# One level of Strassen's product in the odd layer's projections, early products at the layer change, and bias rows by head

## The chip, the core and the metric

The kernel runs on one core of a Trainium2 chip. The metric is the device time of one execution in microseconds; three runs of the kernel before took 2047.49, 2048.87 and 2050.56 us, median 2048.87. Engines: PE multiplies matrices and writes PSUM banks (128 x 512 numbers of 4 bytes); PEld loads the stationary side of a matmul; ACT, DVE and POOL work on elements; SP issues the transfers.

## What is computed

Two layers on 1024 tokens of 1024 features. The first, "even", layer mixes by moving averages, a retention recurrence and an attention over 256 memory rows. The second, "odd", layer is the one that the change rewrites:

```
u = rmsnorm(h, g)
q, kc, vc, ks, vs, kw, vw, gl, xq, gate = split_cols(u @ w_in, ODD_SPLITS)
c = nsa_attention(q, kc, vc, ks, vs, kw, vw, gl, ...)   # 12 heads, 2 groups of k and v
m = mem_attention(xq, mem_n, w_mem_kv)                   # 4 heads
y = concatenate([c, m]) * silu(gate)
return h + y @ w_out
```

The attention `nsa_attention` has three branches per head: over 63 compressed blocks (kc, vc), over the eight best blocks of 64 keys (ks, vs), and over a window of 512 keys (kw, vw), weighted by sigmoids of gl. A bias by distance, read from a small table, is added to the scores. A last rmsnorm gives the output.

## The kernel before

Activations lie transposed, features on the 128 partitions and tokens along the row, in two halves of 512 tokens. Each number is split into two parts, high (rounded to the fast matmul format) and low (the remainder), by `split`: ACT writes the high part (L68) and DVE, or POOL, the remainder (L69). A product of two such numbers takes three matmuls, high by high, high by low, low by high (`mm3`, L75 to L77).

`wload` (L82 to L89) fetches a weight block of 128 output columns, 1024 features deep, in one transfer of 512 KB and splits it whole; it has two buffers. `gemm` multiplies it with the eight feature tiles of u of one half, 8 x 3 matmuls of 128x512, into a bank called mm. `make_u` makes u of one half: it loads eight tiles, multiplies them with gains and the norm, and splits them.

The order: `mem_kv` projects the memory rows for the even layer; the even layer runs half by half and ends in `out_proj` (eight output blocks in two groups of features); u of the odd layer's first half is made; then, for the first half, kc and vc (`cmp_in`), the odd layer's memory projection, k and v (`kv_in`), the bias tables (`rel_tables`), the gate logits (`gates_in`), memory attention with q between (`mem_head`, `q_in`) and gates (`head_gates`); then u of the second half, the first half's memory output (`mem_out`), and the same projections again with `compress` and `select` between. Each weight block is thus fetched and split twice. k and v stay in SBUF, split; v is transposed by PE when it is made. q, gates and compressed probabilities go to DRAM.

`rel_tables` computes a row of 383 bias values for each of 12 heads and writes each row 128 times to DRAM in one transfer (L607), from which each head later reads a skewed table.

The attention then runs 24 units (half, head): `scores` of the next unit, `values` of this one and steps of the output projection `od_out` are interleaved by generators.

The code's order is a priority. A planner places instructions on the engines by its own simulated time, near the order of the code, when their inputs and buffers are free in that simulation. Each engine then runs its queue strictly in the planned order. Memory pools are stacks: a pool that opens takes the place of closed ones, and each of its tiles waits for the last readers of what lay there.

Of the kernel before, what the change touches and what calls it, by code (L numbers as in the profile page):

```python
# [9 lines left out]
F32 = mybir.dt.float32  # L10
# [8 lines left out]
T = 1024  # L19
# [13 lines left out]
HO = 4  # L33
PB = 2
# [4 lines left out]
def net(tc, a, out, dbg=None):  # L39
# [4 lines left out]
    def show(name, ap):  # L44
        if dbg is not None and name in dbg:
            sp.dma_start(dbg[name], ap)

    cst = ctx.enter_context(tc.tile_pool(name="cst", bufs=1))
    uc = ExitStack()
    wp = uc.enter_context(tc.tile_pool(name="wp", bufs=2, side="right"))  # L50
# [3 lines left out]
    pc_ = ExitStack()  # L54
    ps = pc_.enter_context(tc.tile_pool(name="ps", bufs=1, space=PSUM, reuse_waits="tile"))
    banks = {"mm": 3, "s": 2, "t": 2, "o": 1}

    def bank(tag, shape=(128, HT)):
        return ps.tile(list(shape), F32, name="ps_" + tag, tag=tag, bufs=banks[tag])

    def const(name, shape, eng=None):
        t = cst.tile(list(shape), F32, name="c_" + name)
        (eng or sp).dma_start(t, a[name])
        return t
# [9 lines left out]
    def mm3(o, wh, wl, xh, xl, start, stop):  # L74
        pe.matmul(o, wh, xh, start=start, stop=False)  # L75
        pe.matmul(o, wh, xl, start=False, stop=False)  # L76
        pe.matmul(o, wl, xh, start=False, stop=stop)  # L77
# [6 lines left out]
    def wload(src, n=1024, eng=None):  # L84
        r = wp.tile([128, n], F32, name="wr", tag="wr")
        sp.dma_start(r, src)
        h = wp.tile([128, n], F32R, name="wh", tag="wh")
        l = wp.tile([128, n], F32R, name="wl", tag="wl")
        split(h, l, r, eng=eng)  # L89
        return h, l  # L90

    def gemm(o, w, x, nk=8, c=128, start=True, stop=True):
        wh, wl = w
        for k in range(nk):
            mm3(o, wh[:, k * c:(k + 1) * c], wl[:, k * c:(k + 1) * c], x[k][0], x[k][1],
                start and k == 0, stop and k == nk - 1)

    gains = const("gains", (128, 4, 8))
# [9 lines left out]
    def add_square(acc, x, n, first, sq=None):  # L108
        if first:
            act.activation(acc, x, AF.Square)  # L110
        else:
            if sq is None:
                sq = tmp.tile([128, n], F32, name="sq", tag="uf", bufs=2)
            act.activation(sq, x, AF.Square)
            dve.tensor_tensor(acc, acc, sq, OP.add)

    def rstd_of(acc, n, keep=None):
        nt = n // 128
        ss = bank("t")
        for t in range(nt):  # L120
            pe.matmul(ss[:, t:t + 1], acc[:, t * 128:(t + 1) * 128], ones[:, 0:1], start=True, stop=True)
        rs = sm.tile([128, 4], F32, name="rs")
# [5 lines left out]
    def spread(rr, n, raw=False):  # L128
# [10 lines left out]
        r = tmp.tile([128, n], F32, name="rb", tag="rb")  # L139
# [3 lines left out]
    def rstd_rows(acc, n, raw=False):  # L143
        rr = rstd_of(acc, n)
        return spread(rr, n, raw), rr

    def make_u(srcs, n, gi, pool_, tag, rr=None):
# [5 lines left out]
        if rr is None:  # L153
            acc = tmp.tile([128, n], F32, name="acc", tag="acc")
            for k in range(8):
                add_square(acc, load(k), n, k == 0)
            rr = rstd_of(acc, n)
        rb = spread(rr, n)
# [9 lines left out]

    def mem_kv(p_, pre):
        w0 = wload(a[pre + "_mk"][0])  # L170
        acc = p_.tile([128, NMEM], F32, name="macc")
        u = []
        for k in range(8):
            x = p_.tile([128, NMEM], F32, name="mx", tag="mx", bufs=8 if pre == "ev" else 4)
            sp.dma_start(x, a["memT"][k])
            uh = p_.tile([128, NMEM], F32R, name="muh", tag="mu", bufs=16)
            ul = p_.tile([128, NMEM], F32R, name="mul", tag="mu", bufs=16)
            act.activation(uh, x, AF.Copy, scale=gains[:, 3, k:k + 1])
            dve.scalar_tensor_tensor(ul, x, gains[:, 3, k:k + 1], uh.bitcast(F32), OP.mult, OP.subtract)
            add_square(acc, x, NMEM, k == 0)  # L180
            u.append((uh, ul))
        if pre == "ev":
            sp.dma_start(ident, a["ident"])
        rb = None
        kd = [dr.tile([128, NMEM], F32, name=f"{pre}mkd{h}") for h in range(4)]
        vd = [dr.tile([128, HT], F32, name=f"{pre}mvd{m}") for m in range(2)]
        for h in range(4):
            w = w0 if h == 0 else wload(a[pre + "_mk"][h])
            o = bank("mm")
            gemm(o[:, :NMEM], w, u)  # L190
            if rb is None:
                rb, rr = rstd_rows(acc, NMEM)
            t = p_.tile([128, NMEM], F32, name="mkx", tag="mkx", bufs=4)
            act.copy(t, o[:, :NMEM])
            dve.tensor_tensor(t, t, rb, OP.mult)
            sp.dma_start(kd[h], t)
        o2 = [bank("mm"), bank("mm")]
        for c in range(4):
            wh, wl = wload(a[pre + "_mv"][c])
            for kk in range(2):  # L200
                k = 2 * c + kk
                for m in range(2):
                    mm3(o2[m], u[k][0][:, m * 128:(m + 1) * 128], u[k][1][:, m * 128:(m + 1) * 128],
                        wh[:, kk * 512:(kk + 1) * 512], wl[:, kk * 512:(kk + 1) * 512], k == 0, k == 7)
        for m in range(2):
            t = p_.tile([128, HT], F32, name="mvx", tag="mkx", bufs=4)
            act.activation(t, o2[m], AF.Copy, scale=rr[:, m:m + 1])
            sp.dma_start(vd[m], t)
        return kd, vd

    def load_mkv(kv, p_):
# [12 lines left out]
    def mem_att(w, u, mk, mv, h, p_, bufs=1):  # L224
# [35 lines left out]
    def gate_s1(w, u, p_, tag="s1", bufs=3):  # L260
        o = bank("mm")
        gemm(o, w, u)
        th = tmp.tile([128, HT], F32, name="th", tag="th", bufs=2)
# [5 lines left out]
    def make_y(p_, src, s1, scal, tag=None, bufs=0):  # L269
        y = (p_ if tag else tmp).tile([128, HT], F32, name="yf", tag=tag or "t2", bufs=bufs or 2)  # L270
        dve.scalar_tensor_tensor(y, src, scal, s1, OP.mult, OP.mult)
        return y

    def split_y(p_, y, bufs, eng=None, tag="yhl"):
        yh = p_.tile([128, HT], F32R, name="yh", tag=tag, bufs=bufs)
        yl = p_.tile([128, HT], F32R, name="yl", tag=tag, bufs=bufs)
        split(yh, yl, y, eng=eng)
        return yh, yl

    hp_ = [[dr.tile([128, HT], F32, name=f"hp{k}_{f}") for f in range(2)] for k in range(8)]  # L280
    hd = [[dr.tile([128, HT], F32, name=f"hd{k}_{f}") for f in range(2)] for k in range(8)]

    tmp = ctx.enter_context(tc.tile_pool(name="tmp", bufs=1))
    up = uc.enter_context(tc.tile_pool(name="up", bufs=1, side="right", reuse_waits="tile"))

    with tc.tile_pool(name="mk0", bufs=1, reuse_waits="tile") as mp_:
        mkv_ev = mem_kv(mp_, "ev")

    rh = []
    with ExitStack() as ec:  # L290
# [851 lines left out]
```

## Time and profile before

| | us |
|---|---|
| median of three runs | 2048.87 |
| lowest, highest | 2047.49, 2050.56 |
| span of the profiled execution | 2047.5 |
| PE busy in it | 1982.3 |
| DVE, ACT, POOL busy | 1164.9, 904.1, 404.0 |

The profiled execution's own time is its span, 2047.5 us from the first to the last instruction, 1.4 below the median. Matmuls are pipelined: one lasts longer than the distance to the next, and the groups' busy times add up overlaps. The price of a matmul in a gapless row is the distance between two starts. The granted clock is the share of full speed that PE was allowed.

### The profile page before, as it was taken

Reading aid. Unit: us, or ns where it says so; the run is one execution under the profiler, and the core shown is the slowest. Engines: PE = TensorE matmul, PEld = TensorE weight load, DVE = VectorE, ACT = ScalarE, POOL = GpSimd, SP = SyncE. Lnnn points to the kernel's source line nnn. Section 1 sums busy time; section 2 is a strip of 40 time slices with the busy share of each in tenths; the row PEclk is TensorE's granted clock in tenths of the full one; section 3 lists DMA queues with packets and bytes.
Section 4 is the critical chain, followed back from the end, with each engine's and each line's share of the span. In section 5 each row is a group of like instructions: output and inputs, shape, how many; then the busy total and the mean of one; then the engine's idle time right before and its main releaser. Section 6 shows DMA issues by size and latency. Waiting matters only on the chain.

```text
span 2047.5 us, 28222 instructions
## 1 busy us (share of the span) xinstructions
PE 1982.3 (97%) x10070; PEld 1657.5 (81%) x10070; DVE 1164.9 (57%) x2494; ACT 904.1 (44%) x1656; POOL 404.0 (20%) x478
## 2 busy tenths in 40 slices
PE   7999999999999999959999999999999999999996
PEld 6788888888888878748887888788788888888885
DVE  6674455746445573314444237744576677867675
ACT  5444222434421253313333222333576677767674
POOL 0130110013011000000002114300343444433422
PEclk9999999999999999979999999999899999999998
DMA  7433243632224365454356657444534532151312
GB/s 249 143 98 112 83 134 114 211 106 83 96 79 133 114 213 158 120 89 134 121 173 206 221 178 230 143 119 133 180 120 144 164 110 62 53 165 46 114 37 93
DMA packets 124051, 270.30 MB, mean 132 GB/s; under 512 B 15079, under 2 KB 31847, under 8 KB 123879
## 3 DMA queue, kind: packets, MB, share of 16 engines
q1 hardware_dynamic: 123912, 268.51, 42.5%
q8 instruction: 79, 1.29, 0.3%
q14 instruction: 60, 0.49, 0.1%
HBM read 217.87 MB, written 50.59 MB: 131 GB/s over the span
## 4 chain that ended last, share of the span: by engine, by line
PE 88%; DVE 4%; DMA 4%; issue 1%; ACT 1%; SPq 1%; POOL 0%; DVEq 0%; ACTq 0%; POOLq 0%
PE ps_mm L77 20%; PE ps_mm L75 20%; PE ps_mm L76 20%; PE ps_t L106 6%; PE ps_s L75 3%; PE ps_s L77 3%; PE ps_s L76 3%; PE ps_o L82 2%; PE ps_o L80 2%; PE ps_o L81 2%; PE ps_s L703 1%; DMA mkr<-odmkd 1%; DVE wl L69 1%; PE ps_o L75 1%; ACT wh L68 1%
## 5 line engine op out<-in xcount | busy, mean ns | idle before, releaser
L75 PE MATMUL ps_mm<-uh,wh 128*128 128x512 f32 (+1 forms) x1360 | 538.4, 396 | 25.8 <-ACT wh L68 25.6
L68 ACT CAST wh<-wr 128x1024 fp32r<-128x1024 f32 (+1 forms) x286 | 270.1, 947 | 631.3 <-PE ps_mm L76 505.2
L77 PE MATMUL ps_mm<-uh,wl 128*128 128x512 f32 (+1 forms) x1360 | 537.0, 395 | 3.3 <-DVE wl L69 3.3
L76 PE MATMUL ps_mm<-ul,wh 128*128 128x512 f32 (+1 forms) x1360 | 537.2, 395 | 1.2 <-DVE ul L69 1.2
L69 DVE TENSOR_TENSOR wl<-wr,wh 128x1024 fp32r<-128x1024 f32 (+2 forms) x222 | 277.7, 1251 | 348.5 <-ACT wh L68 347.5
L75 PEld LDWEIGHTS ps_mm<-uh,wh 128*128 128x128 f32 (+1 forms) x1360 | 255.5, 188 | 80.2 <-ACT wh L68 27.2
L77 PEld LDWEIGHTS ps_mm<-uh,wl 128*128 128x128 f32 (+1 forms) x1360 | 255.4, 188 | 58.4 <-DVE wl L69 5.6
L76 PEld LDWEIGHTS ps_mm<-ul,wh 128*128 128x128 f32 (+1 forms) x1360 | 255.4, 188 | 54.6 <-DVE ul L69 2.0
L77 PE MATMUL ps_mm<-yh,wl 128*128 128x512 f32 x512 | 206.9, 406 | 1.2 <-POOL wl L69 1.2
L75 PE MATMUL ps_mm<-yh,wh 128*128 128x512 f32 x512 | 204.1, 405 | 2.4 <-ACT yh L68 1.4
L76 PE MATMUL ps_mm<-yl,wh 128*128 128x512 f32 x512 | 205.1, 401 | 0.0
L69 DVE TENSOR_TENSOR apl<-ps_t,aph 128x512 fp32r<-128x512 f32 x204 | 136.2, 671 | 48.4 <-ACT aph L68 40.2
L69 POOL TENSOR_TENSOR wl<-wr,wh 128x512 fp32r<-128x512 f32 x64 | 84.5, 1324 | 383.0 <-PE ps_mm L76 295.1
L68 ACT CAST aph<-ps_t 128x512 fp32r<-128x512 f32 x204 | 114.3, 567 | 79.4 <-PE ps_o L81 41.7
L918 POOL TENSOR_TENSOR Pw<-Pw,arc 128x640 f32<-128x640 f32 (+2 forms) x96 | 97.3, 1014 | 141.0 <-DVE arc L914 67.8
L77 PEld LDWEIGHTS ps_mm<-yh,wl 128*128 128x128 f32 x512 | 96.7, 189 | 23.1 <-POOL wl L69 2.5
L75 PEld LDWEIGHTS ps_mm<-yh,wh 128*128 128x128 f32 x512 | 95.9, 189 | 23.0 <-ACT wh L68 2.0
L76 PEld LDWEIGHTS ps_mm<-yl,wh 128*128 128x128 f32 x512 | 96.9, 189 | 20.0 <-DVE yl L69 0.6
L910 ACT ACTIVATE Ps<-Ps,anm 128x512 f32<-128x512 f32 (+3 forms) x96 | 74.6, 777 | 33.4 <-DVE anm L907 33.0
L922 ACT ACTIVATE Ps<-Ps,arc 128x512 f32<-128x512 f32 (+3 forms) x96 | 74.5, 776 | 19.1 <-DVE arc L914 18.3
L106 PE MATMUL ps_t<-c_ident,Ps 128*128 128x128 f32 x432 | 67.9, 274 | 0.4 <-ACT Ps L922 0.4
L910 ACT ACTIVATE Pw<-Pw,anm 128x640 f32<-128x640 f32 (+2 forms) x96 | 65.6, 683 | 0.0
(316 smaller groups left out, 3297.0 us busy)
## 6 DMA issues: line engine op xcount, KB each, us to landing
wr<-in_ev_gate SPq DMA_DIRECT2D x32, 512.0 KB, 3.5
wr<-in_ev_out SPq DMA_DIRECT2D x32, 512.0 KB, 3.7
wr<-in_od_gate SPq DMA_DIRECT2D x32, 512.0 KB, 3.9
wr<-in_od_out SPq DMA_DIRECT2D x64, 256.0 KB, 3.0
oa<-oho SPq DMA_DIRECT2D x52, 256.0 KB, 2.2
oxr<-oa SPq DMA_DIRECT2D x52, 256.0 KB, 2.9
wr<-in_od_q SPq DMA_DIRECT2D x24, 512.0 KB, 3.6
x<-in_xT SPq DMA_DIRECT2D x32, 256.0 KB, 4.3
```

Source lines behind the costliest of these rows:

```text
L68: act.copy(hi, src)
L69: (eng or dve).tensor_tensor(lo, src, hi.bitcast(F32), OP.subtract)
L75: pe.matmul(o, wh, xh, start=start, stop=False)
L76: pe.matmul(o, wh, xl, start=False, stop=False)
L77: pe.matmul(o, wl, xh, start=False, stop=stop)
L80: pe.matmul(o, wh, xh, start=start, stop=False)
L81: pe.matmul(o, wl, xh, start=False, stop=False)
L82: pe.matmul(o, wh, xl, start=False, stop=stop)
L106: pe.transpose(o, x, ident[:k, :k])
L910: act.activation(pt, pt, AF.Exp, bias=nm[:, bi:bi + 1], accum_out=su[:, bi:bi + 1])
L918: pool.tensor_tensor(pt, pt, rc[:, bi:bi + 1].to_broadcast(list(pt.shape)), OP.mult)
L922: act.activation(pt, pt, AF.Copy, scale=rc[:, bi:bi + 1])
```

## The change

The odd layer's u of both halves is seen as a 2 x 2 matrix of blocks: B11 and B21 are the upper and lower 512 features of the first half, B12 and B22 those of the second. Two weight blocks of 128 columns (two heads) are likewise four blocks of 512 features. Instead of eight block products, seven are formed, from sums of blocks (Winograd's order of Strassen's product). The sums of u, T1 to T4, are made once; four sums of the weights, for each pair, on POOL. Products are added up in PSUM banks a, b and c, partly read out to SBUF between and combined there; results go to DRAM. All 22 pairs of blocks (6 q, 6 of k and v, 2 xq, 8 gate) go this way.

```diff
+    def u_sums(U, uo, x):
+        for k in range(4):
+            b11, b12, b22 = x[0][k], x[1][k], x[1][k + 4]
+            dve.tensor_tensor(b11, b12, b11, OP.subtract)
+            pool.tensor_tensor(b12, b22, b12, OP.subtract)
+            dve.tensor_tensor(b22, b22, b11, OP.subtract)
+            split(*U["T2"][k], b22)
...
+    def product(o, w, x, start):
+        for k in range(4):
+            c = slice(k * 128, (k + 1) * 128)
+            mm3(o, w[0][:, c], w[1][:, c], x[k][0], x[k][1], start and k == 0, k == 3, not start)
...
+    def strassen(U, sa, sb, sink, p_, scale=1.0, p1d=None):
...
+        pool.tensor_tensor(S[0], rb[:, lo], rb[:, hi], OP.add)
+        pool.tensor_tensor(S[1], S[0], ra[:, lo], OP.subtract)
+        pool.tensor_tensor(S[2], ra[:, lo], rb[:, lo], OP.subtract)
+        pool.tensor_tensor(S[3], ra[:, hi], S[1], OP.subtract)
...
+        pa = bank("a")
+        if p1d is None:
+            product(pa, whl(ra[:, lo]), U["B11"], True)
+            p1 = held(pa, "p1")
+            pc = bank("c")
+            product(pc, whl(ra[:, hi], pool), U["B21"], True)
+            done(0, 0, pc, p1)
+        else:
+            p1 = hold("p1")
+            sp.dma_start(p1, p1d)
+        product(pa, whl(S[1]), U["T2"], p1d is not None)
+        u2 = held(pa, "u2")
+        flush()
+        product(pa, whl(S[2]), U["T3"], False)
+        u3 = held(pa, "u3")
+        pb = bank("b")
+        product(pb, whl(S[0]), U["T1"], True)
+        done(1, 1, pb, u3)
+        product(pa, whl(rb[:, hi], pool), U["T4"], False)
...
+        def last():
+            product(pb, s4, U["B22"], False)
+            done(0, 1, pb, u2)
+
+        pending.append(last)
```

`held` copies a bank to SBUF (on ACT; on DVE, adding the first product, where that was held in DRAM), `done` adds a bank and a held tile on DVE and hands the result to a store or to the gate's tanh. `flush` issues the seventh product of the pair before. A weight is now fetched whole (`wraw`) and split in pieces of 512 (`whl`), of which five are buffered; the even layer's `wload` splits its 1024 in two pieces as well.

At the layer change, u of the first half is made before the even layer's last output projection, and then, while u of the second half is not there, the first two products of six pairs are formed from B11 and B21; the first is stored, the sum of both is a result:

```diff
+    ahead = [("kc", 0), ("vc", 0), ("q", 0), ("q", 2), ("q", 4), ("q", 6)]
...
+            kd[nm, i] = early(U, a["od_" + nm][i], sink,
...
+            if n == 0:
+                for k in range(8):
+                    sp.dma_start(X[1][k], hd[k][1])
+                    sp.dma_start(X[0][k], xd[k])
+        drain(mem_kv("od", None, u_late(uo), wtile("mrb")[:, :NMEM]))
+        u_half(U, X, 1, 1, rh[1], wtile("rb"))
+        u_sums(U, uo, X)
```

`mem_kv` now fetches the memory rows in two transfers through the weight buffers. The order of the odd layer becomes: pairs kc, vc, q 0, `rel_tables`, q 2, `compress`, q 4, the gate logits (for the second half from B11, T1 and B22), q 6 to 10, xq, `select`, gates 12 and 14, ks, and then kw, vs, vw and the gates 0 to 10 with a step of the memory attention before each. `mem_out` goes; its work is a generator in the attention stage. The bias rows go to DRAM once and are spread there, two heads at a time between pairs:

```diff
-                sp.dma_start(frd, fr[:, None, :383].to_broadcast([12, 128, 383]))
+            sp.dma_start(frs, fr)
...
+    def rel_rows(i):
+        for h in (2 * i, 2 * i + 1):
+            sp.dma_start(frd[h], frs[h:h + 1, :383].to_broadcast([128, 383]))
```

k and v are fetched from DRAM, split and transposed at the attention's start, group 0 before the first unit's scores and group 1 behind them:

```diff
+    def kv_prep(g):
+        for f in range(2):
...
+                k = fetch(tmp, zo["k" + br][g][f], "uf", 2, "kraw")
+                split(KT[br, g][0][:, c], KT[br, g][1][:, c], k)
+                v = fetch(tmp, zo["v" + br][g][f], "uf", 2, "vraw")
+                b = bank("t", (128, 4, 128))
+                for n in range(4):
+                    transpose(b[:, n], v[:, n * 128:(n + 1) * 128])
...
-        proj = [od_out(at, 1, {}, 0, (12, 13, 14, 15))]
+        proj = [od_out(at, f, {}, 0, (12, 13, 14, 15)) for f in range(2)]
```

The PSUM banks are laid out anew for the even layer, the pairs and the attention, and smaller buffers (in `compress` and `select` single instead of double) make room.

More of the change, by code (lines that the diff above doesn't have):

```diff
@@ L106, in transpose, with add_square @@
         pe.transpose(o, x, ident[:k, :k])
-    def add_square(acc, x, n, first, sq=None):
+    def add_square(acc, x, n, first, eng=None):
         if first:
@@ L126, in rstd_of, with spread @@
         return rr
-    def spread(rr, n, raw=False):
+    def spread(rr, n, raw=False, r=None):
         nt = n // 128
@@ L145, in rstd_rows, with u_pool, u_late, u_half @@
         return spread(rr, n, raw), rr
+    U_ORDER = ("T3", "T1", "T2", "B22", "B21", "B11", "T4")
+    def u_pool(uo, names=U_ORDER[:-1]):
+        return {nm: [[uo.tile([128, HT], F32R, name=f"{nm}{k}{s}", tag=f"{nm}{k}{s}") for s in "hl"] for k in range(4)]
+                for nm in names}
+    def u_late(uo):
+        return [[uo.tile([128, HT], F32R, name=f"T4{k}{s}", tag=f"T4{k}{s}") for s in "hl"] for k in range(4)]
+    def u_half(U, x, gi, f, rr, rb):
+        rb = spread(rr, HT, r=rb)
+        for k in range(8):
+            dve.scalar_tensor_tensor(x[f][k], x[f][k], gains[:, gi, k:k + 1], rb, OP.mult, OP.mult)
+            if f == 0 or k >= 4:
+                split(*U[("B11", "B21", "", "B22")[2 * f + k // 4]][k % 4], x[f][k])
@@ new lines, in product, with early @@
+    def product(o, w, x, start):
+        for k in range(4):
+            c = slice(k * 128, (k + 1) * 128)
+            mm3(o, w[0][:, c], w[1][:, c], x[k][0], x[k][1], start and k == 0, k == 3, not start)
+    pending = []
+    def early(U, sa, sink, hold, out_t, scale=1.0):
+        ra = wraw(sa)
+        pa = bank("a")
+        product(pa, whl(ra[:, :HT], pool), U["B11"], True)
+        t = hold()
+        act.activation(t, pa, AF.Copy, scale=scale)
+        pc = bank("c")
+        product(pc, whl(ra[:, HT:], pool), U["B21"], True)
+        d = dr.tile([128, HT], F32, name=f"p1d{len(kept)}")
+        kept.append(d)
+        sp.dma_start(d, t)
+        c = out_t()
+        dve.scalar_tensor_tensor(c, pc, scale, t, OP.mult, OP.add)
+        sink(0, 0, c, None)
+        return d
@@ new lines, in load_mkv @@
+    def load_mkv(kv, h, p_, bufs):
+        mk = p_.tile([128, 2, NMEM], F32R, name="mk", tag="mk", bufs=bufs)
+        mv = p_.tile([128, 2, 2, 128], F32R, name="mv", tag="mv", bufs=bufs)
+        t = p_.tile([128, 2, NMEM], F32, name="mkr", tag="xq", bufs=2)
+        sp.dma_start(t[:, 0], kv[0][h])
+        for m in range(2):
+            sp.dma_start(t[:, 1, m * 128:(m + 1) * 128], kv[1][m][:, h * 128:(h + 1) * 128])
+        split(mk[:, 0], mk[:, 1], t[:, 0])
+        v = t[:, 1].rearrange("p (m d) -> p m d", m=2)
+        split(mv[:, :, 0], mv[:, :, 1], v)
+        return mk, mv
@@ L167, in make_u, with load_mkv4 @@
         return u
[L169 to L211, printed above, removed]
+    def load_mkv4(kv, p_):
         mk = p_.tile([128, 4, 2, NMEM], F32R, name="mk", tag="mk")
@@ new lines, in net @@
+    wpx.close()
+    wpx = ExitStack()
+    cur["wp"] = wpx.enter_context(tc.tile_pool(name="wp", bufs=1, side="right", reuse_waits="tile"))
+    cur.update(wn=1024, wr=2, wh=5, ws=4, hs=4, sc=3, th=1)
+    uox = ExitStack()
+    uo = uox.enter_context(tc.tile_pool(name="uoA", bufs=1, side="right", reuse_waits="tile"))
+    U = u_pool(uo, ("B11", "B21"))
+    rb = spread(rh[0], HT, r=tm2.tile([128, HT], F32, name="rb", tag="rb"))
+    for k in range(8):
+        x = ep.tile([128, HT], F32, name="x0", tag="pa", bufs=3)
+        sp.dma_start(x, hd[k][0])
+        dve.scalar_tensor_tensor(x, x, gains[:, 1, k:k + 1], rb, OP.mult, OP.mult)
+        split(*U[("B11", "B21")[k // 4]][k % 4], x)
+        sp.dma_start(xd[k], x)
@@ L560, in od_out @@
                 if ct == 0:
-                    acc = tmp.tile([128, HT], F32, name="facc", tag="acc")
+                    acc = cur["late"].tile([128, HT], F32, name="facc", tag="acc")
                 add_square(acc, t, HT, ct == 0)
@@ new lines, in gates_in @@
+    def gates_in(p_):
+        w = wload(a["od_gl"], 288)
+        for f in range(2):
+            o = bank("s")
+            if f == 0:
+                gemm(o[:36], w, U["B11"] + U["B21"], c=36)
+            else:
+                gemm(o[:36], w, U["B11"], nk=4, c=36, stop=False)
+                gemm(o[:36], w, U["T1"], nk=4, c=36, start=False, stop=False)
+                gemm(o[:36], w, U["B22"], nk=4, c=36, start=False, k0=4)
+            gt = tmp.tile([36, HT], F32, name="gt", tag="uf", bufs=2)
```

814 lines of the change are left out of this document (487 added, 327 removed).

## The prediction

> **What bounds the kernel now.** I read the page's totals and its chain of waits first, then the busy time by stage, then the places where PE stood still.
>
> ```profile
> span 2047.5 us, 28222 instructions
> PE 1982.3 (97%) x10070; PEld 1657.5 (81%) x10070; DVE 1164.9 (57%) x2494; ACT 904.1 (44%) x1656; POOL 404.0 (20%) x478
> PE 88%; DVE 4%; DMA 4%; issue 1%; ACT 1%; SPq 1%; POOL 0%; DVEq 0%; ACTq 0%; POOLq 0%
> ```
>
> PE is busy 1982.3 of 2047.5 us and carries 88% of the chain. So PE work that is taken away counts in full wherever the stage around it is gapless. The next view, busy time in chosen stretches, says where it is (columns: stretch, length, then busy us and instructions of PE, PEld, DVE, ACT, POOL, granted clock, DMA share, GB/s).
>
> ```profile
> 0.00:60.00 60.00, 45.51 (x209) 35.68 (x210) 37.45 (x70) 32.89 (x58) 2.12 (x10) 0.97 0.79 252
> 60.00:735.00 675.00, 674.29 (x3162) 560.98 (x3162) 383.63 (x610) 241.59 (x388) 87.70 (x70) 1.00 0.36 114
> 735.00:830.00 95.00, 94.00 (x456) 77.77 (x456) 50.62 (x78) 38.59 (x58) 2.63 (x2) 1.00 0.65 203
> 883.00:925.00 42.00, 19.11 (x76) 15.55 (x75) 5.34 (x8) 5.12 (x9) 0.00 (x0) 0.67 0.57 105
> 1095.00:1120.00 25.00, 22.70 (x94) 17.05 (x93) 12.98 (x17) 7.03 (x11) 8.78 (x7) 1.00 0.78 242
> 1230.00:1310.00 80.00, 78.94 (x450) 68.30 (x449) 66.68 (x126) 23.80 (x36) 40.09 (x46) 1.00 0.64 199
> 1310.00:1436.00 126.00, 125.47 (x593) 104.03 (x592) 60.57 (x111) 46.63 (x89) 2.58 (x2) 1.00 0.43 129
> 1436.00:1456.00 20.00, 16.94 (x60) 12.98 (x59) 10.87 (x39) 11.49 (x30) 6.78 (x12) 0.74 0.61 198
> 1456.00:2005.00 549.00, 545.25 (x3216) 468.43 (x3215) 392.81 (x1216) 379.27 (x785) 220.33 (x298) 1.00 0.34 103
> ```
>
> The even layer (60 to 735) loses 0.71 us, the attention (1456 to 2005) 3.75 us: nothing is to be had there except work. PE stands still at the start (14.5 us of 60) and between 883 and 925 (22.9 us). The projections that the change rewrites lie from about 760 to 1436, and outside that hole they are gapless: even at 1230 to 1310, with DVE busy 66.68 of 80, PE lost only 1.06 us.
>
> **Term 1: fewer matmuls.** The odd layer projects 44 blocks of 128 columns (12 q, 12 of k and v, 4 xq, 16 gate) for two halves of the tokens, each in 8 x 3 matmuls of 128x512: 44 x 2 x 24 = 2112. After it are 22 pairs with 7 products of 4 x 3 matmuls: 22 x 7 x 12 = 1848. 264 go. A single matmul's duration overlaps the next, so the price is the distance of starts in a gapless row (timeline of PE, first and last of 14 matmuls):
>
> ```profile
> 1433.72 0.39 PE L76 MATMUL ps_mm<-ul,wh 128*128 128x512 f32 x1
> ...
> 1436.66 0.39 PE L77 MATMUL ps_mm<-uh,wl 128*128 128x512 f32 x1
> ```
>
> (1436.66 - 1433.72) / 13 = 0.2262 us; 264 x 0.2262 = **-59.7 us**. The busy column's 0.39 us would make it 103 us and be wrong. The Trainium skill, "TensorE: Matmul & The Clock Gate", section "Back-to-back issue gap", gives about 131 ns sustained and 215.7 ns isolated for 512 columns; as estimates by that page the term would be -34.6 or -56.9 us. No row here comes near 131 ns, so the measurement decides.
>
> **Term 2: the bias rows.** In the chain of waits the hole is one load of the memory keys, and the list of DMA issues shows what was in front of it.
>
> ```profile
> frd<-fr SPq DMA_DIRECT2D x1, 2298.0 KB
> 882.38 3.88 SPq L86
> 886.32 23.60 DMA mkr<-odmkd
> 890.00:895.00 5.00, 4.29 (x19) 3.21 (x18) 0.00 (x0) 0.00 (x0) 0.00 (x0) 1.00 0.68 81
> ...
> 915.00:920.00 5.00, 2.82 (x9) 2.44 (x10) 2.68 (x4) 3.16 (x6) 0.00 (x0) 0.50 0.23 51
> 920.00:925.00 5.00, 5.00 (x26) 4.31 (x25) 1.81 (x2) 1.16 (x3) 0.00 (x0) 0.93 0.84 299
> ```
>
> One issue of 2298 KB from twelve partitions moves at 70 to 80 GB/s, 31 us, and the small load behind it takes 23.60 us. Between the rows shown, 895 to 915, PE does nothing. Lost: 0.71 + 20 + 2.18, and at the low clock 2.82 x 0.5 + 5 x 0.07 = 1.8, together 24.7. Afterwards one row of 12x384 goes out and is spread in six calls of two heads, each behind a pair's loads, and the memory keys come much later. I take **-24.7 us**. Two heads are 383 KB; at the same 74 GB/s a call lasts 5.2 us, hidden by a pair of 84 x 0.2262 = 19.0 us of PE whose next weights have two buffers.
>
> **Term 3: what goes with the old order.** The second half's u (1095 to 1120, 2.3 us lost, with the weights of the output projection late) and the old layer change (735 to 830, 1.0 us) vanish: **-3.3 us**. The 96 matmuls of that half's memory output projection move into the attention and cost there what they cost here.
>
> **Term 4: added PE work.** The gate logits of the second half need 12 instead of 8 row blocks (B11, T1 and B22 instead of u): 12 more matmuls of 36 columns, spaced alike:
>
> ```profile
> 865.95 0.40 PE L75 MATMUL ps_mm<-uh,wh 128*36 128x512 f32 x1
> ...
> 868.04 0.40 PE L75 MATMUL ps_mm<-uh,wh 128*36 128x512 f32 x1
> ```
>
> 2.09 / 9 = 0.232; x 12 = **+2.8 us**.
>
> **Term 5: the pairs.** Prices, from the groups by form and the DMA issues:
>
> ```profile
> L68 ACT CAST wh<-wr 128x512 fp32r<-128x512 f32 x64 | 38.9, 616 | 44.8 <-PE ps_mm L76 16.6 <-DMA wr<-in_od_out 16.3 <-issue 7.9
> L620 ACT COPY kcx<-ps_mm 128x512 f32<-128x512 f32 x8 | 4.6, 579 | 0.0
> L556 DVE TENSOR_TENSOR oho<-ps_mm,oxr 128x512 f32<-128x512 f32 x64 | 43.7, 688 | 31.2 <-PE ps_mm L77 25.4 <-DMA oxr<-hd 4.6 <-DMA oxr<-oa 1.1
> L115 DVE TENSOR_TENSOR facc<-facc,sq 128x512 f32<-128x512 f32 x14 | 13.8, 983 | 8.0 <-ACT sq L114 7.9
> L115 DVE TENSOR_TENSOR acc<-acc,sq 128x512 f32<-128x512 f32 x14 | 9.6, 687 | 0.8 <-ACT sq L114 0.5
> L69 POOL TENSOR_TENSOR wl<-wr,wh 128x512 fp32r<-128x512 f32 x64 | 84.5, 1324 | 383.0 <-PE ps_mm L76 295.1 <-ACT wh L68 70.5 <-PE ps_mm L77 15.1
> wr<-in_od_q SPq DMA_DIRECT2D x24, 512.0 KB, 3.6
> aq<-qd SPq DMA_DIRECT2D x24, 256.0 KB, 2.8
> ```
>
> For 19.0 us of PE a pair asks: POOL 4 sums and 2 remainders, 6 x 1.32 = 7.9 us; ACT 7 splits at 0.62 and up to 3 copies at 0.58 (6.1), in a gate pair 4 tanh more (8.4); DVE 5 remainders at 0.69 and 4 combinations at 0.69 (6.2), in a gate pair 4 more (9.0). Weight loads fall from 88 of 512 KB to 44, and 6 for the early products; SP gains 46 stores of 256 KB (16 of k and v, 8 xq, 8 gates, 8 rows of u, 6 held products) and as many fetches later; with 38 fewer loads of 512 KB the queues carry less, under gapless PE. All engines stay under half of 19.0, so on average PE bounds. But bank a is read out after the third and the fourth product before the next may write it, and b has a single buffer. The order puts one other product, 12 x 0.2262 = 2.7 us, behind each of these reads (0.58 on ACT, 0.69 on DVE), and selection and memory attention share the queues in front of them. Bounds: nothing, as 1310 to 1436 (0.5 us in 126), and all three bare, 22 x (0.58 + 0.58 + 0.69) = 40.7 us. Nearest are the two gapless rows: 1.06 in 80 with DVE dense gives 22 x 19.0 / 80 x 1.06 = 5.5. I take **+5**.
>
> DVE's addition of two SBUF tiles took 983 ns in one group and 687 in another of the same shape. The Trainium skill, "GPSIMD Engine Reference", section "1. Specifications", says that GpSimd shares its SBUF interfaces with VectorE, and names contention with DVE instructions of two SBUF inputs. By that rule the five remainders of a pair would take 0.98, DVE 1.5 us more per pair; that alone stays hidden, yet it speaks against me where a read stands behind such a remainder.
>
> **Term 6: the layer change.** The first half's u is made under the last output projection (8 x 24 matmuls, 43.4 us); the twelve early products (32.6 us) and the odd memory projection (96 matmuls of 256 and 48 of 512 columns, 96 x 0.1131 + 48 x 0.2262 = 21.7 us) then cover the second half's load, u, and the sums: DVE 8 x 0.79 scalings and some 26 operations at 0.7, about 25 us, POOL about 16 us, loads of 4 MB (at 203 GB/s, the rate of the row from 735, 20 us). Behind them wait T2, then T3, T1, T4.
>
> ```profile
> L162 DVE SCALAR_TENSOR_TENSOR uf<-x,c_gains,rb 128x512 f32<-128x512 f32 x32 | 24.1, 790 | 2.0 <-ACT rb L140 2.0
> ```
>
> That is 25 of 54 us, early enough by half. What stays open is the change of weight buffers and banks, twice. If the cover went, these 25 us would come; the old change lost 1.0. I take **+4**.
>
> **Term 7: the start.** The memory rows now come through the two weight buffers, so the first key weights load only after four conversions and four squares:
>
> ```profile
> 4.91 1.04 ACT L68 CAST wh<-wr 128x1024 fp32r<-128x1024 f32 x1 [2.89 <-DMA wr<-in_ev_mk]
> 6.27 0.40 ACT L110 ACTIVATE macc<-mx 128x256 f32<-128x256 f32 x1
> L178 ACT ACTIVATE muh<-mx,c_gains 128x256 fp32r<-128x256 f32 x16 | 7.7, 498 | 5.3 <-DMA mx<-in_memT 5.3
> ```
>
> 4 x (0.50 + 0.40) + a load of 3.6 = about 7 us later; but in the first 60 us PE idles 14.5 anyway and splits of half a weight release matmuls earlier. Bounds -1 and +8; **+3**.
>
> **Term 8: into the attention.** K and V of a head group are now fetched from DRAM, split, V transposed, through two buffers. The last pair's banks and hold tiles must be read first (0.7), then K is split (0.62 + 0.69), the window's K is fetched into the freed buffer (2.8) and split (1.3), and the first scores follow: some 7 us without PE, then part load.
>
> ```profile
> 1440.00:1445.00 5.00, 3.35 (x13) 2.40 (x12) 2.43 (x9) 2.78 (x7) 2.61 (x3) 0.80 0.91 292
> 1445.00:1450.00 5.00, 5.00 (x17) 3.93 (x17) 3.35 (x16) 3.76 (x10) 1.19 (x3) 0.50 0.80 290
> ```
>
> Before, this place lost 3.1 us idle and some 4.4 at the low clock (20 x 0.74 granted). I take 7 + 2 at half clock + 3 of part load = 12 against 7.5: **+4**. Bounds: 0, and +17 if all eight fetches (two at a time, 4 x 4.1 us) come before the first score.
>
> **Sum.** 2047.5 - 59.7 - 24.7 - 3.3 + 2.8 + 5 + 4 + 3 + 4 = 1978.6. The median of the runs lies 1.4 above the profiled span: **1980**.
>
> **Rivals.** (B) The reads in term 5 are bare, 40.7 instead of 5: 2016. For it: ACT, which does half of them, is a queue in order, and its splits wait for buffers; against it: 2.7 us of cover against 0.6. (D) The bias rows don't do what the change says: the DRAM rows of 1532 bytes run no faster, and the weights behind them are late again, 24.7 us: 2005. Against it: no consumer of rows or weights is near. (C) Slower: the weights' chain is bare. A pair's first product (the second factor S1) waits for rb's load 3.6, two dependent POOL sums 2.6, split 1.3: 7.5 us. If the last split that frees rb runs only when its product is due, each pair waits: 22 x 7.5 = 165, 2145. It turns slower than before from (2048.9 - 1980) / 22 = 3.1 us per pair. Against it: five split buffers let that split run four products, 10.9 us, ahead.
>
> **Chances.** Forecast 0.62, alone from 1958 to 2002 by the bounds of terms 6 to 8; B 0.17; D 0.11; C 0.10, of which 0.02 land within 0.2%. A measurement of this kernel tells about 0.2% from no change. Faster 0.90, same 0.02, slower 0.08. The range 1958 to 2016 leaves out C, the upper part of B and a gain beyond the bounds.
>
> **What would show it.** Right: PE starts 0.226 apart through all pairs with under 1 us lost in each; no hole of 20 us around the memory attention; PE's busy sum near 1982 - 57 = 1925; a hole of some 7 us with a half clock before the first scores. Wrong: PE waiting on ACT or DVE reads of banks a and b (B), on POOL sums (C), on weights while bias rows move (D), or a layer change that costs 20 us.

## The result and the profile after

The changed kernel takes 2075.30 us (median of four runs, 2074.93 to 2075.86) against 2048.18 for the kernel before (four runs, 2046.15 to 2050.56). The ratio is 1.0124, 95% interval [1.0108, 1.0140]: it is slower by 27 us. The forecast was 1980 us, range 1958 to 2016.

The page of the kernel after, its span, its totals and the shares of the chain:

```profile
span 2073.1 us, 28764 instructions
PE 1945.5 (94%) x9814; PEld 1618.8 (78%) x9814; DVE 1281.2 (62%) x2729; ACT 943.2 (45%) x1867; POOL 614.2 (30%) x627
PE 48%; DVE 4%; POOL 2%; DMA 2%; issue 1%; ACT 1%; SPq 0%; DVEq 0%; POOLq 0%; ACTq 0%
```

PE's busy time did fall, from 1982.3 to 1945.5, and the span rose all the same: PE's idle time went from 65.2 (2047.5 - 1982.3) to 127.6 us. To say where the time went I cut each span into stretches of 5 us, leaving out the last, shorter one, and took for each the idle time of PE plus its busy time times (1 - granted clock). Two of the 414 rows of the kernel after (columns as in the prediction):

```profile
875.00:880.00 5.00, 0.69 (x1) 0.30 (x2) 1.90 (x4) 0.78 (x2) 3.50 (x3) 0.96 0.28 107
...
915.00:920.00 5.00, 3.11 (x6) 1.01 (x4) 5.00 (x4) 1.86 (x3) 5.00 (x4) 0.50 0.00 0
```

The last one loses 1.89 + 3.11 x 0.50 = 3.4 us. Summed by place, idle and clock together:

| place (us in the kernel after) | before | after | difference |
|---|---|---|---|
| start, 0 to 75 | 18.1 | 39.5 | +21.4 |
| between the even halves, 425 to 450 | 0.0 | 18.1 | +18.1 |
| layer change, 760 to 945 (before: 735 to 830) | 1.0 | 57.4 | +56.4 |
| hole at the bias rows (before: 870 to 930) | 26.4 | none | -26.4 |
| projections, 945 to 1425 (before: 930 to 1425) | 3.9 | 8.2 | +4.3 |
| start of the attention, 1425 to 1500 | 8.1 | 18.3 | +10.2 |
| the rest | 17.9 | 17.8 | -0.1 |
| sum | 75.3 | 159.2 | +83.9 |

What PE did at full speed is its busy time less the clock loss: 1982.3 - 12.6 = 1969.7 before, 1945.5 - 34.7 = 1910.8 after. That is -58.9 us of work, and +83.9 of losses; the two give +25.0 where the spans differ by 25.6, and the stretches left out hold the rest. So the work went away as it should, and three new holes, 95.9 us together, took more than all of it.

PE's waits in these three places, kernel after (columns: waiting engine and line, for whom, us in total, times, longest):

```profile
PE ps_t L134 <- DVE acc L128: 14.6, 1, 14.6
PE ps_t L134 <- DVE macc L128: 13.8, 1, 13.8
```

```profile
PE ps_t L134 <- DVE acc L128: 10.2, 1, 10.2
PE ps_t L154 <- DVE dg L149: 2.3, 1, 2.3
```

```profile
PE ps_b L77 <- ACT T10h L70: 8.4, 1, 8.4
PE ps_b L78 <- POOL T11l L71: 6.3, 1, 6.3
PE ps_b L78 <- DVE T10l L71: 5.2, 1, 5.2
PE ps_t L154 <- DVE dg L149: 4.4, 1, 4.4
```

The first fence is 0 to 75, the second 425 to 450, the third 760 to 945. At the start before, the longest waits were 6.4 (`muh`) and 4.6 (`wh`), and between the even halves there was none. In the first two holes PE waits for a sum of squares: the norm that must be known before u can be made. In the third it waits for T1, a sum of u. None of these works is large. They begin late.

**Why they begin late.** The timeline of ACT in the kernel after, around the second hole:

```profile
422.20 0.63 ACT L127 ACTIVATE sq<-ho 128x512 f32<-128x512 f32 x1 [0.34 <-DVE ho L563]
...
427.80 0.63 ACT L127 ACTIVATE sq<-ho 128x512 f32<-128x512 f32 x1 [0.34 <-DVE ho L563]
428.33 0.61 ACT L127 ACTIVATE sq<-x 128x512 f32<-128x512 f32 x1
```

`sq<-ho` squares the even layer's output of the first half; the last of these can only come when PE has made the last output block. `sq<-x` squares the input rows of the second half, which depends on nothing of that. Yet the first comes 0.5 us after the last. Both write to `sq`, and `sq` is one of two buffers of a scratch tag. In the kernel before, the squares of the even output had a buffer of their own (`hsq`), and the last square of the second half's input was done at 156 us:

```profile
155.50 0.64 ACT L114 ACTIVATE sq<-x 128x512 f32<-128x512 f32 x1
```

The edit is one argument of one call, which the core of the diff shown above leaves out:

```diff
-                        add_square(acc, t, HT, ct == 0, ep.tile([128, HT], F32, name="hsq", tag="hsq"))
+                        add_square(acc, t, HT, ct == 0)
```

The same happened to the results of the memory projection (four own buffers before, `mkx` and `mvx`): now they lie in the same two scratch buffers, with the squares, the diagonal of the norm (`dg`), and the scaled tiles of u (`uf`). Buffers of one tag are handed out in the code's order, so a work of a later stage waits until the earlier stages' works have held and released theirs. At the start the profile names this wait. The squares of the first half's input stand behind the store of `mvx`, the end of the even layer's memory projection (ACT, kernel after):

```profile
45.39 1.26 ACT L336 ACTIVATE mvx<-ps_s,rrkm 128x512 f32<-128x512 f32 x2
49.33 2.02 ACT L127 ACTIVATE sq<-x 128x512 f32<-128x512 f32 x3 [2.17 <-DMA evmvd<-mvx]
```

At the layer change, ACT and DVE of the kernel after:

```profile
874.51 1.26 ACT L336 ACTIVATE mvx<-ps_s,rrkm 128x512 f32<-128x512 f32 x2 [5.04 <-PE ps_s L79]
```

```profile
877.36 1.90 DVE L149 TENSOR_SCALAR dg<-c_ident,rrk 128x128 f32<-128x128 f32 x4 [7.12 <-issue]
881.74 6.39 DVE L177 SCALAR_TENSOR_TENSOR x<-x,c_gains,rb 128x512 f32<-128x512 f32 x8 [2.48 <-ACT rb L157]
```

`mvx`, the end of the odd memory projection, stands in front of `dg`, the start of the second half's u. But the memory projection is the work that was to cover this u. The last load of its tiles was issued at 821 us and such loads take 5.3 us (the issue on SP's queue, and the list of DMA issues from 780 to 830, with the median time to landing):

```profile
821.14 0.32 SPq L796 DMA_DIRECT2D x<-hd  x1
```

```profile
x<-hd SPq DMA_DIRECT2D x8, 256.0 KB, 5.3
```

The tiles then lay there for some 50 us. The releaser of `dg` reads "issue", so here the profile names none. The times fit the same cause: the two stores of `mvx` are issued from 875.22 us on and take 2.1 us to land (median, list of DMA issues from 870 to 882), and `dg` starts at 877.36. The run `own_od` below tests it.

### The profile page after: what moved, and what is told of

Read it like the earlier page. It is cut to its first block, busy times and chain, and to the rows that moved or that the text cites. A ratio compares the mean times of both kernels' runs of the same rounds, so it can differ in the third digit from the quotient of the medians.

```text
span 2073.1 us, 28764 instructions
## 1 busy us (share of the span) xinstructions
PE 1945.5 (94%) x9814; PEld 1618.8 (78%) x9814; DVE 1281.2 (62%) x2729; ACT 943.2 (45%) x1867; POOL 614.2 (30%) x627
## 3 DMA queue, kind: packets, MB, share of 16 engines
q1 hardware_dynamic: 131556, 271.53, 40.7%
q8 instruction: 77, 1.26, 0.3%
## 4 chain that ended last, share of the span: by engine, by line
PE 48%; DVE 4%; POOL 2%; DMA 2%; issue 1%; ACT 1%; SPq 0%; DVEq 0%; POOLq 0%; ACTq 0%
PE ps_t L120 5%; PE ps_a L77 3%; PE ps_a L78 3%; PE ps_a L79 3%; PE ps_s L77 3%; PE ps_s L79 3%; PE ps_s L78 3%; PE ps_mm L79 3%; PE ps_mm L77 3%; PE ps_mm L78 3%; PE ps_o L84 2%; PE ps_o L82 2%; PE ps_o L83 2%; PE ps_b L77 2%; PE ps_b L79 2%; PE ps_b L78 2%
## 5 line engine op out<-in xcount | busy, mean ns | idle before, releaser
L70 ACT CAST wh<-wr 128x512 fp32r<-128x512 f32 (+1 forms) x395 | 242.2, 618 | 474.5 <-PE ps_mm L78 304.4
L71 DVE TENSOR_TENSOR wl<-wr,wh 128x512 fp32r<-128x512 f32 (+1 forms) x281 | 208.1, 745 | 175.9 <-ACT wh L70 168.9
L77 PE MATMUL ps_mm<-uh,wh 128*128 128x512 f32 x640 | 253.2, 398 | 2.7 <-ACT uh L70 2.7
L79 PE MATMUL ps_mm<-uh,wl 128*128 128x512 f32 x640 | 252.9, 395 | 0.0
L78 PE MATMUL ps_mm<-ul,wh 128*128 128x512 f32 x640 | 252.6, 395 | 0.0
L71 POOL TENSOR_TENSOR wl<-wr,wh 128x512 fp32r<-128x512 f32 x114 | 150.0, 1318 | 325.7 <-ACT wh L70 270.4
L77 PEld LDWEIGHTS ps_mm<-uh,wh 128*128 128x128 f32 x640 | 121.1, 190 | 28.3 <-ACT uh L70 4.4
L78 PEld LDWEIGHTS ps_mm<-ul,wh 128*128 128x128 f32 x640 | 121.1, 189 | 24.6 <-DVE ul L71 0.5
L79 PEld LDWEIGHTS ps_mm<-uh,wl 128*128 128x128 f32 x640 | 120.9, 189 | 24.6
L71 DVE TENSOR_TENSOR wl<-ws,wh 128x512 fp32r<-128x512 f32 x88 | 71.2, 811 | 40.8 <-ACT wh L70 37.6
```

The source lines that it names most:

```text
L70: act.copy(hi, src)
L71: (eng or dve).tensor_tensor(lo, src, hi.bitcast(F32), OP.subtract)
L77: pe.matmul(o, wh, xh, start=start, stop=False, skip_group_check=skip)
L78: pe.matmul(o, wh, xl, start=False, stop=False, skip_group_check=skip)
L79: pe.matmul(o, wl, xh, start=False, stop=stop, skip_group_check=skip)
```

## The experiments

All ratios are against the kernel before, run on the same chip.

**Own buffers, one set at a time, and all three.** `own_hsq` gives the squares of the even output a buffer of their own again, `own_ev` and `own_od` the results of the even and of the odd memory projection, `own_all` all of them. The arithmetic, the order of the code and the Strassen products stay.

```diff
-                        add_square(acc, t, HT, ct == 0)
+                        add_square(acc, t, HT, ct == 0, sq=ep.tile([128, HT], F32, name="hsq", tag="hsq"))
...
-            t = tmp.tile([128, HT], F32, name="mkx", tag="uf", bufs=2)
+            t = own.tile([128, HT], F32, name="mkx", tag="mkx", bufs=nb) if own else tmp.tile([128, HT], F32, name="mkx", tag="uf", bufs=2)
```

> Only the square of the even layer's output gets its own buffer. Shared-scratch theory: the hole between the even halves goes, 13 us idle and some 3 at the half clock, so 2059; the wait of PE for acc at about 425 us is no more. Rival (the pieces of 512 make the even layer's splits late): nothing moves, 2075.

> Only the even layer's memory projection gets own buffers for its results. Shared-scratch theory: the wait for acc of 14.6 us at 45 to 60 us and the half clock behind it go, 13 to 18 us, so about 2060. Rival (memory rows through the two weight buffers delay the first matmul): the first matmul stays at 14 us and at most 5 us are gained, 2070.

> Only the odd layer's memory projection gets own buffers for its results, so the second half's u may be prepared under it. Shared-scratch theory: preparation starts near 825 instead of 877 us, and 45 to 50 us of the hole at 875 to 930 go, 2028. Rival (DVE and POOL hold each other up in the sums, 1.7 us per operation instead of 0.7 and 1.3): the preparation takes longer under the cover and at most half of it is hidden, 20 to 25 us, 2052.

> The changed kernel with three own scratch buffers in place of the two that it shares under the tag uf: for the memory projections' results (mkx, mvx) of both layers and for the square of the even layer's output (hsq). Nothing else differs. Shared-scratch theory: the three holes at the start (0 to 75 us), between the even halves (425 to 445) and at the layer change (875 to 930) go to the size they had before; together 70 to 90 us, so about 1990. Rival, the weight buffers of the memory rows and the layer change's own chain of sums: the holes stay, within 10 us of 2075.

| kernel | median us | ratio, 95% interval | PE idle at the start | between the halves | at the layer change |
|---|---|---|---|---|---|
| before | 2048.18 | 1 | 15.0 | 0.0 | 1.0 |
| after | 2075.30 | 1.0124 [1.0108, 1.0140] | 34.2 | 13.1 | 43.4 |
| own_hsq | 2065.25 | 1.0097 [1.0074, 1.0119] | 34.7 | 3.4 | 41.7 |
| own_ev | 2054.20 | 1.0048 [1.0027, 1.0070] | 19.0 | 12.6 | 40.9 |
| own_od | 2057.73 | 1.0054 [1.0038, 1.0070] | 34.2 | 12.8 | 28.1 |
| own_all | 2025.32 | 0.9899 [0.9879, 0.9919] | 19.3 | 3.4 | 28.0 |

The last three columns are PE's idle time in us, in the places of the table above, which lie somewhat earlier in the faster kernels. The clock loss is left out, because it differs between profiles where the idle time does not: at the layer change it is 14.0 us in the kernel after and 20.6 in `own_hsq`.

Each edit shortens the hole that it was made for, by 9.7, 15.2 and 15.3 us, and leaves the other two. All three together take 40.0 us of idle time away. The total times are compared by their ratios, since the kernel before took 2046.08 us in the set of these four runs. Against the kernel after, `own_hsq` gains 6 us, `own_ev` 16, `own_od` 14 and `own_all` 46; the single gains in time add up to somewhat less, while those in idle time agree. For `own_hsq` the intervals overlap, so its gain is shown by its place and not by its time. With buffers alone the change turns from 1.2% slower to 1.0% faster, but not to the 1990 us that were expected. In `own_all` the waits for `acc` are gone from the first two places (0 to 75, then 400 to 440):

```profile
PE ps_t L135 <- DVE macc L129: 13.8, 1, 13.8
```

```profile
PE ps_t L155 <- DVE dg L150: 2.8, 1, 2.8
```

With the clock, `own_all` loses 22.1 us at the start, 6.4 between the halves and 40.4 at the layer change (730 to 915), where the kernel after loses 39.5, 18.1 and 57.4. So the first two holes have this one cause for the most part, and the third has another one beside it: `own_od` was expected at 2028. In `own_od` u of the second half does begin earlier, its scalings start at 837 instead of 882 us, and PE's waits for T1 are gone. In their place PE waits for results of the early products, which DVE combines (`sc`), and for split weights (735 to 945):

```profile
PE ps_c L77 <- DVE sc L218: 11.8, 3, 8.5
PE ps_a L77 <- ACT wh L70: 7.0, 2, 4.7
```

The rival that was written down for `own_od`, that DVE and POOL hold each other up in the sums, comes next.

**The sums on DVE alone.** In the kernel after, DVE and POOL in the third hole:

```profile
894.68 0.68 DVE L71 TENSOR_TENSOR T10l<-x,T10h 128x512 fp32r<-128x512 f32 x1
895.28 0.68 DVE L71 TENSOR_TENSOR T12l<-x,T12h 128x512 fp32r<-128x512 f32 x1
897.77 1.09 DVE L71 TENSOR_TENSOR wl<-ws,wh 128x512 fp32r<-128x512 f32 x1 [1.82 <-ACT wh L70]
...
907.16 1.76 DVE L186 TENSOR_TENSOR x<-x,x 128x512 f32<-128x512 f32 x1
908.85 1.75 DVE L71 TENSOR_TENSOR T20l<-x,T20h 128x512 fp32r<-128x512 f32 x1
...
923.97 0.68 DVE L71 TENSOR_TENSOR T43l<-x,T43h 128x512 fp32r<-128x512 f32 x1
```

```profile
876.10 1.26 POOL L232 TENSOR_TENSOR ws<-ws,wr 128x512 f32<-128x512 f32 x1
...
888.27 8.81 POOL L234 TENSOR_TENSOR ws<-wr,ws 128x512 f32<-128x512 f32 x1 [2.68 <-DVE x L177]
897.05 4.60 POOL L185 TENSOR_TENSOR x<-x,x 128x512 f32<-128x512 f32 x3
...
906.65 1.72 POOL L231 TENSOR_TENSOR ws<-wr 128x512 f32<-128x512 f32 x1
908.34 1.71 POOL L71 TENSOR_TENSOR T31l<-x,T31h 128x512 fp32r<-128x512 f32 x1
```

An operation of DVE on two tiles in SBUF takes 0.68 us while POOL stands still or is held, and 1.76 while POOL works; one of POOL takes 1.26 alone and 1.72 beside DVE. From 907 on both start once in 1.69 us (908.85 - 907.16, 908.34 - 906.65): one of each per turn, which is nearly the sum of the two alone, so they take turns and do not run side by side. The operation at 888.27 was held for 8.81 us, while DVE ran one such operation behind another; it ended at 897.08, in the first gap of DVE (895.96 to 897.77). The Trainium skill, "SBUF — State Buffer", section "SBUF: two separate sides", calls the ports that the two share an exclusive lock, kept for the whole instruction by whoever starts first. These rows agree with it.

`own_all_dve` is `own_all` with all sums of u on DVE:

```diff
-            pool.tensor_tensor(b12, b22, b12, OP.subtract)
+            dve.tensor_tensor(b12, b22, b12, OP.subtract)
...
-            split(*U["T3"][k], x[1][k], eng=(dve, pool)[k % 2])
+            split(*U["T3"][k], x[1][k], eng=dve)
```

> As own_all, and the sums of u and their remainders wholly on DVE, none on POOL. In own_all PE still idles some 14 us at 815 to 835 while DVE and POOL work side by side at 1.7 us an operation. Theory that the two engines hold each other up: DVE's operations return to 0.7 us, the preparation gets shorter though DVE has 16 operations more, 8 to 15 us less than own_all, 2010 to 2017. Rival, that DVE's amount of work delays the memory projection's splits: 5 us more than own_all, 2030.

Measured: 2021.21 us, ratio 0.9875 [0.9855, 0.9895]. By the ratios that is 5 us less than `own_all`, where 8 to 15 were expected, and the intervals overlap, so that no gain in time is shown. In its profile DVE's operations are short again, as here among the sums:

```profile
817.33 0.68 DVE L186 TENSOR_TENSOR x<-x,x 128x512 f32<-128x512 f32 x1
```

But the preparation did not get shorter: from the first scaling to the last remainder of T2 it takes 34.3 us, against 32.9 in `own_all`. With POOL's share of the sums on DVE the time is about the same, which fits two engines that take turns. At the layer change PE idles for 24.5 instead of 28.0 us (730 to 915). With the clock the place loses 29.7 instead of 40.4, but 7.2 of these 10.7 us are clock loss. PE's waits there (735 to 905, first `own_all`, then `own_all_dve`):

```profile
PE ps_c L77 <- DVE sc L219: 7.1, 2, 4.6
PE ps_a L77 <- ACT wh L70: 6.7, 2, 4.7
PE ps_s L77 <- ACT wh L70: 6.7, 1, 6.7
```

```profile
PE ps_a L77 <- ACT wh L70: 5.9, 2, 4.4
PE ps_s L77 <- ACT wh L70: 4.2, 1, 4.2
PE ps_c L77 <- DVE sc L219: 4.2, 3, 2.0
```

So the turn-taking is there, but most of the third hole stays open without it. The traces show two other things in this place. First, `sc` and the conversions of the memory rows stand behind u in DVE's queue; in `own_all` SP waited 8.0 and 4.6 us for two of these conversions before it could fetch the next weights into their buffers. Second, the longest wait for `wh`, 4.7 and 4.4 us, belongs to the first pair behind the memory projection. In `own_all` POOL's first sum of its weights starts when their load has landed, at 867.22 us, and the first matmul, after two sums and a split, at 870.53. That is the weights' chain of rival C, bare once instead of 22 times. No run separates the two.

**The converse.** `bef_shared` is the kernel before with its squares of the even output and its results of the memory projections in the two scratch buffers. Nothing of the Strassen products is in it.

```diff
-                        add_square(acc, t, HT, ct == 0, ep.tile([128, HT], F32, name="hsq", tag="hsq"))
+                        add_square(acc, t, HT, ct == 0)
...
-            t = p_.tile([128, NMEM], F32, name="mkx", tag="mkx", bufs=4)
+            t = tmp.tile([128, HT], F32, name="mkx", tag="uf", bufs=2)[:, :NMEM]
```

> The kernel before, whole in its work; its squares of the even output (own buffer before) and its results of the memory projections (four own buffers before) go into the scratch of two buffers that the changed kernel also uses for them. Nothing of the Strassen products is in it. Theory of the shared scratch: the first two of the three holes come back without the change: at the start about +15 to +22 us (PE idle of 0 to 75 us from 17 towards 39), at the even layer's change of halves +10 to +18; the third does not, because no work on the second half waits at the layer change here. Together +20 to +40, ratio 1.010 to 1.020. Rival, that the holes belong to the order of work that the product brings (the memory rows through the weight buffers at the start, the planner's placing): within 5 us of before, ratio 0.998 to 1.002.

Measured: 2088.44 us, ratio 1.0204 [1.0182, 1.0226], just above the upper end of what was expected. The waits at the two places (0 to 75, then 415 to 455) are those of the kernel after, to within 0.4 us:

```profile
PE ps_t L121 <- DVE acc L115: 14.7, 1, 14.7
```

```profile
PE ps_t L121 <- DVE acc L115: 10.6, 1, 10.6
PE ps_t L138 <- DVE dg L133: 2.3, 1, 2.3
```

So the scratch alone makes these two holes; the products and their order are not needed for them. Of the 40 us, 16.5 were lost at the start, 18.5 between the halves, and, which was not expected, 6.5 at the layer change (the same sums by place).

**The bias rows alone.** `bef_rows` is the kernel before with only the bias rows changed.

```diff
-                sp.dma_start(frd, fr[:, None, :383].to_broadcast([12, 128, 383]))
+                sp.dma_start(frs, fr)
...
+        def rel_rows(i):
+            for h in (2 * i, 2 * i + 1):
+                sp.dma_start(frd[h], frs[h:h + 1, :383].to_broadcast([128, 383]))
```

> The kernel before with one part of the change alone: the bias rows go to DRAM once and are spread two heads at a time, between the q blocks of the second half. Theory: the hole of PE at 890 to 917 us and the half clock behind it go, 24.7 us, 2022 against 2047. Rival, that another transfer or the weights take the place of the wait: less than 12 us.

Measured: 2027.09 us, ratio 0.9905 [0.9884, 0.9925]: -20 us. Its profiled span is 2022.0, and where 22.9 us of PE were idle before, the rows are now

```profile
885.00:890.00 5.00, 5.00 (x24) 4.14 (x23) 0.42 (x1) 0.41 (x1) 0.00 (x0) 1.00 0.82 246
890.00:895.00 5.00, 2.55 (x12) 1.77 (x10) 0.85 (x2) 1.54 (x3) 0.00 (x0) 1.00 0.16 50
895.00:900.00 5.00, 4.70 (x24) 3.69 (x25) 4.02 (x5) 2.57 (x5) 0.00 (x0) 1.00 0.55 177
```

In the kernel after, a call for one head lands after 6.6 us in the median, and no hole stands behind it:

```profile
frd<-frs SPq DMA_DIRECT2D x12, 191.5 KB, 6.6
```

This part of the change does what it says. By itself it beats the whole change.

**Without the seventh product.** `no_last` leaves the seventh product of each pair out, 264 matmuls more, so the second half of each pair's first block is not computed.

```diff
-            product(pb, s4, U["B22"], False)
```

> The changed kernel without the seventh product of each pair: 22 x 12 = 264 matmuls of 128x512 fewer, so the second half of the first block of every pair is not computed (splits, sums and the combination stay). Theory that PE bounds the pairs: 264 x 0.2262 = 59.7 us less, 2015 against 2075. Rival, that weights, POOL sums or the read-outs bound them: less than half of it, over 2045.

Measured: 2041.51 us, ratio 0.9975 [0.9961, 0.9990]. By the ratios that is 31 us less than the kernel after, about half of the 59.7 and between the two expectations. PE's work at full speed fell by what the price per matmul says: busy 1898.6 less clock loss 46.8 is 1851.8, and 1910.8 - 1851.8 = 59.0 us for 264 matmuls, 0.223 us each. But the losses grew by 25.5 us, 17.5 of it in the pairs, from 8.2 to 25.7 (945 to 1385). There PE's idle time rose from 5.8 to 18.5 us, and two new waits make up 11.3 of these 12.7 us:

```profile
PE ps_s L933 <- DMA w<-in_cmp_w: 6.8, 1, 6.8
PE ps_a L77 <- ACT wh L70: 4.5, 1, 4.5
```

With seven products PE bounds the pairs nearly throughout. With six, the load of the weights of `compress` and one split come out from under PE's work, and they, with the losses outside the pairs, took back about half of the saving.

**Two steps on the way to a faster kernel.** `own_all_dve_mem` is `own_all_dve` with the memory rows in own buffers, not through the weights' buffers; `own_all_kv` is that, with the raw values at the attention's start in two other buffers than the raw keys, so that four fetches are under way.

```diff
-                r = wraw(a["memT"][k:k + 4].rearrange("k p m -> p k m"))
+                r = rows.tile([128, 1024], F32, name="mr", tag="mr", bufs=2)
+                sp.dma_start(r.rearrange("p (k m) -> p k m", k=4), a["memT"][k:k + 4].rearrange("k p m -> p k m"))
...
-                v = fetch(tmp, zo["v" + br][g][f], "uf", 2, "vraw")
+                v = fetch(at0, zo["v" + br][g][f], "t2", 2, "vraw")
```

> As own_all_dve, and the memory rows get own buffers instead of the two weight buffers, in both layers. Theory of term 7: the first matmul moves from 14 us back to 7 us, and 3 to 8 us are gained at the start, 2 to 4 at the layer change: about 2005. Rival, that the start is bound by the transfers anyway: within 2 us of own_all_dve.

> The kernel with all own buffers, the sums of u on DVE and the memory rows in own buffers; beside that the raw values v of the attention's start are fetched into two other buffers than the raw keys, four fetches under way instead of two. Theory: the start of the attention (about 17 us lost between 1370 and 1430) is bound by fetches two at a time, eight in four turns of about 4 us; with four at a time half of the turns go: -5 to -9 us against the same kernel without it, ratio to the kernel before 0.981 to 0.984. Rival: the splits and the transposes behind the fetches, or the DMA queues, set it: within 2 us, ratio 0.985 to 0.987.

Measured: 2017.36 us, ratio 0.9858 [0.9831, 0.9885], and 2013.05 us, ratio 0.9836 [0.9818, 0.9854]. About 2005 was expected of the first, and -5 to -9 us of the second step. Each step's gain is within the intervals, so neither is shown by itself. For the memory rows the profile shows what took the place: the wait at the start, 13.8 for `macc`, has become one for the first weights' split,

```profile
PE ps_s L77 <- ACT wh L70: 11.7, 1, 11.7
```

For the keys and values the loss at the attention's start hardly moved (16.9 us in `own_all_dve_mem`, 16.2 in `own_all_kv`, summed by 5 us from 1360 to 1430); the wait for keys has become one for the first unit's q, whose fetch now stands behind the values (first `own_all_dve_mem`, then `own_all_kv`):

```profile
PE ps_s L77 <- ACT ks0h L70: 4.4, 1, 4.4
```

```profile
PE ps_s L77 <- ACT aqh L70: 7.0, 1, 7.0
```

Together with the buffers and the sums, though, this last kernel beats both: 1.6% below the kernel before and, by the ratios, 59 us below the change as made.

## Why the prediction was wrong, point by point

- **Terms 1 and 4** (-59.7 and +2.8) were right: -56.9 forecast, -58.9 measured at full speed, and `no_last` gives 0.223 us for a matmul where the prediction had 0.2262. The distance of starts was the right price.
- **Term 2**, the bias rows, was right in its mechanism: -24.7 forecast, -20.0 measured alone, with 15 to 24 in the interval; 4.4 us of the hole's place stay lost. The calls are slower than priced, 6.6 us for one head where 5.2 stood for two, but no wait of PE in the pairs is for them or for weights behind them. Rival D falls with it.
- **Term 3** vanished as said, but the old layer change's 1.0 us was the smallest part of what the new one costs.
- **Term 5**, the pairs, was right: +5 forecast, 8.2 lost against 3.9 before, +4.3. Rival B (40.7) and rival C (165) did not come: a slower kernel did, but by another mechanism than the one priced for it.
- **Term 6** failed, in two steps. It put the second half's u at "25 of 54 us, early enough by half", under the early products and the memory projection, and took +4. The first step took the cover as given because the data were there early. They were (821); the scratch buffer was not, until the cover itself was done (874.51). 57.4 us were lost, and own buffers (`own_all`) take back 17.0 of them. The second step counted u as hidden once it ran under the cover. In `own_all` it does run there, and the place still loses 40.4 us: cover and u share DVE's queue, so u delays the cover's own `sc` and conversions, and the first pair's weights come bare. DVE's 25 and POOL's 16 us were also laid side by side, and the runs show that they take turns: in the kernel after, from the diagonal at 877.36 to the last remainder of T4 at 924.65, are 47 us, with sums and splits of weights between. The page of the Trainium skill that the prediction named beside term 5, "GPSIMD Engine Reference", section "1. Specifications", with its contention between the two engines, bore on this place, where DVE and POOL were densest, and there it was not asked. `own_all_dve` says that this alone was not the price. The prediction's own sign of being wrong, a layer change that costs 20 us, came.
- **Term 7**, the start, failed in the same way as the first step of term 6: +3 forecast, bounds to +8, and +21.4 measured. What was priced, the rows through the weights' buffers, was right: with own scratch (`own_all`) the start loses some 4 us more than before. The other 17 are the shared scratch.
- **The even layer** was no term at all. The prediction said of it "nothing is to be had there except work", and a stage in which nothing is to be gained can still lose: +18.1, of which one argument of one call made 11.7. The 6.4 that `own_all` still loses there were not taken apart.
- **Term 8** was undersized: +4 forecast, +10.2 measured, within its bounds (0 to +17). Its bottleneck is not settled by `own_all_kv`.
- **The range** was not added up from the bounds that it names. Terms 6 to 8 reach by theirs from 1968 us (0, -1 and 0) to 2019 (25, 8 and 17), not from 1958 to 2002; neither end reaches 2075.

In short, two steps failed: the move of tiles from buffers of their own into a shared tag was counted as nothing, without asking who waits for a slot of it, and the second half's u was counted as hidden by work that uses the same engine. Between forecast (-68.9 against the span before) and outcome (+25.6) lie 94.5 us. The shared tag is 46 of them by `own_all` (17.4 at the start, 11.7 between the halves, 17.0 at the layer change), and the rest of the layer change 36.4 (40.4 - 4). The 6.4 between the halves are left, and 5.6 for all other terms. So own buffers alone would not have brought the forecast: `own_all`, at 2025 us, still lies above its range.

What stays open: even in `own_all_dve` the layer change loses 29.7 us. Its waits point at DVE's queue, in which u of the second half stands in front of what the cover needs, and at the first pair's weights. No run took that apart.

## What to carry to other kernels

A scratch tag is a queue: its buffers are given out in the order of the code, so list for each tag who takes a slot, in order, and ask of each later taker whether it was to run ahead of an earlier one. Before work is counted as hidden, look not only whether its data are there but whether its buffers and its engine are free then, above all when the cover itself writes into the same tag or needs the same engine. And work divided between DVE and POOL, each with two tiles in SBUF, was not halved here: add the two up.

## What the hardware showed

Two things were not expected in their size. DVE and POOL, both with two tiles in SBUF, took turns: 0.68 against 1.76 us and 1.26 against 1.72, and one operation of POOL stood 8.81 us until DVE paused. And short work between waits ran at half the clock: in the row from 915 to 920 of the kernel after PE was busy for 3.11 of 5 us at a granted clock of 0.50. The layer change lost 14.0 us by the clock beside 43.4 by waiting.
